# Six weight buffers and four row buffers in the u part of a PEER block, and gate table groups of 16 tokens

## The chip, the cores and the metric

The kernel runs on one core of one Trainium2 chip. The metric is device time in microseconds (us) of one execution. Each kernel has a median over several runs, and one further execution was profiled; all rows come from that one.

## The reference, cut to what matters

The layer is a hybrid attention block (forgetting attention and mLSTM, left out here) followed by PEER, a retrieval over 16384 single-neuron experts. The change is in the PEER half, for 512 tokens of width 2048 in four tiles of 128.

```
D_MODEL, SEQ, PEER_HEADS, PEER_TOPK, PEER_N_KEYS = 2048, 512, 8, 16, 128

def peer_ffn(x, w_q, keys, u, v):                       # x: T=512 tokens x 2048
    q = (xt @ w_q).reshape(T, PEER_HEADS, 2, PEER_KEY_DIM // 2)
    scores = jnp.einsum('thpd,pnd->thpn', q, keys)
    s_top, i_top = lax.top_k(scores, PEER_TOPK)
    cand = s_top[:, :, 0, :, None] + s_top[:, :, 1, None, :]
    s_fin, pos = lax.top_k(cand.reshape(T, PEER_HEADS, 256), PEER_TOPK)
    idx = ...                                           # 8 x 16 = 128 experts per token
    gate = jax.nn.softmax(s_fin, axis=-1)
    act = gelu(sum over d of u[idx] * x) * gate         # u part
    return sum over the 128 experts of act * v[idx]     # v part
```

## The kernel before, in words

**Two ways through PEER.** Tile 0 (128 tokens) and the first 64 tokens of tile 1 go the sparse way: for each of 128 + 64 steps a gather fetches one row of `u` for each of 128 partitions (1 MB, `gathered`, L639, issued on POOL), and VectorE makes its dot product with the token (`dot`, L649). The other 320 tokens go the dense way: all 128 blocks of 128 experts are multiplied with them on TensorE (`early_steps`, tile `sacc`). One block streams two chunks of `uT` (512 KB each), 48 matmuls, a Gelu (tile `es`) and a write to the DRAM table `stab`. Each chunk goes through `stream_split`: SP loads it into `raw` (4 buffers), ScalarE rounds it to `hi` (L117), VectorE makes the remainder `lo` (L119), 3 buffers each. The matmuls take `hi`, then `lo`.

**The gate table.** `table` turns indices and gates of the 384 tokens of tiles 1 to 3 into a table `gtab` in DRAM, `TG` = 32 tokens at a time. I call the work on four tokens a quad: one compare on VectorE (`on`, L949), four scalings on ScalarE (`og`, L954, 6 buffers), matmuls into `gp_` (four calls, eight instructions in the trace), and one copy on ScalarE into `stg` (L957, two buffers). After every 8 quads ScalarE issues the write of `stg` to `gtab` (L961). A quad stands beside three steps of `early_steps`, 18 `sacc` matmuls. Ten groups (80 quads beside 30 blocks) come before the sparse way is done, two groups (16 quads beside 6 blocks) after it, since they need its result.

**Pace.** `advance(n)` runs the sparse steps from inside the dense ones: 1.25 steps per block at first, 1.6 beside the first ten groups (`PACE_G`), and then over 26 blocks as many as are left of `U_STEPS`. A gather is followed by its dot `LAG` = 2 steps later; the pool `rows` has 3 buffers. `beside` makes a gather and a dot wait for the ScalarE `hi` cast that is current in program order.

**The order.** The builder arranges each engine's instructions ahead of time (`lo` with a priority, `AHEAD_LO`), and each engine, SP and POOL too, runs its list strictly in order.

**The stages by time.** To about 920 us attention, output projection and queries; 920 to 963 the end of tile 0's queries (`w_q0`, which reads `x30T`) and its top-k on VectorE; 963 to 1475 queries of the other tiles with 56 blocks; 1515 to 1830 the ten table groups; 1830 to 2045 the 26 blocks with the dense gathers; 2045 to 2110 the last two groups; 2110 to 2200 the last blocks and the loads of gates for the v part (`load_gates`, `gated`, tiles `gtA`, `gtB`); then the v part.

Of the kernel before, what the change touches and what calls it, by code (L numbers as in the profile page):

```python
# [20 lines left out]
P = 128  # L21
# [21 lines left out]
TG = 32  # L43
# [10 lines left out]
LAG = 2  # L54
AHEAD_LO = 35
U_STEPS = SLOTS + S1 + 2 * LAG + 1
# [33 lines left out]
def block_kernel(ctx: ExitStack, tc: tile.TileContext, a, out):  # L90
# [16 lines left out]
    pace = [None]  # L107

    def stream_split(src, width=1024, to=None):
        raw = stream.tile([P, 1024], F32, tag="raw", name="raw", bufs=4)  # L110
# [520 lines left out]
    def gathered(src, idx, n, use, ready):  # L631
        ahead = []
        for j in range(n + LAG):
# [3 lines left out]
            if j < n:  # L637
                row = rows.tile([P, D], F32, tag="row", name="row")
# [4 lines left out]
            if j >= LAG:  # L643
                beside(use(ahead.pop(0), j - LAG))
# [53 lines left out]
    with ExitStack() as rx:  # L698
# [203 lines left out]
        xt0.close()  # L902
        steps = itertools.chain(*[early_steps() for _ in range(EARLY_0)])
# [26 lines left out]
    with ExitStack() as rx:  # L930
# [9 lines left out]
        def table(tg, blocks):  # L940
            stg = n3.tile([P, NI, TG], F32, tag="stg", name="stg")
            steps = itertools.chain(*[early_steps() for _ in range(blocks)])
            for q4 in range(TG // 4):
                for _ in range(blocks):
                    next(steps)
# [6 lines left out]
                for q in range(4):  # L952
# [5 lines left out]
                               in_=gp_)  # L958
            for _ in steps:
                pass  # L960
            nc.scalar.dma_start(out=gtab[tg], in_=stg.rearrange("p i q -> p (i q)"))  # L961

        pace_u[0] = PACE_G
        for tg in range(NS // TG, NTG):
            table(tg, EARLY_G)
# [12 lines left out]
        for tg in range(NS // TG):  # L978
            table(tg, EARLY_G)
# [192 lines left out]
```

## Time and profile before

| | |
|---|---|
| median of 3 runs | 3234.92 us (3233.81 to 3237.32) |
| profiled execution, its own time | 3235.63 us |
| its span, first to last instruction | 3233.8 us |
| TensorE (PE) busy | 3124.3 us, 97% |
| VectorE (DVE) busy | 2324.0 us, 72% |
| ScalarE (ACT) busy | 1277.9 us, 40% |
| mean granted TensorE clock | 0.989 |

The span is 1.8 us less than the execution's own time; the profiled execution lies 0.7 us above the median. Busy PE counts matmuls that overlap in its pipeline, so a stretch in which PE is busy may still run slower than at its best; the number of matmuls in a stretch tells that.

### The profile page before, as it was taken

How to read it: one execution, taken by the hardware profiler on the slowest of the kernel's cores; microseconds unless marked ns; L12 is line 12 of the kernel's file. 1: busy time of each engine (PE TensorE's matmuls, PEld its weight loads, DVE VectorE, ACT ScalarE, POOL GpSimd, SP SyncE). 2: the span in 40 equal slices, each digit the busy share in tenths (PEclk: the TensorE clock that was granted, in tenths of full speed). 3: DMA queues.
4: the chain of work that ended last, by engine and by line, in shares of the span. 5: the costliest groups of instructions: out<-in, count | busy, mean ns of one | idle time of the engine just before them, and what ended most of it. 6: DMA issues, size and time to landing. Idle time of an engine off the chain costs nothing.

```text
span 3233.8 us, 43256 instructions
## 1 busy us (share of the span) xinstructions
PE 3124.3 (97%) x16682; PEld 2746.8 (85%) x16682; DVE 2324.0 (72%) x3251; ACT 1277.9 (40%) x1955; POOL 593.8 (18%) x444
## 2 busy tenths in 40 slices
PE   8999999998989999999999899999999999999998
PEld 6788787787779999999989888997888888888887
DVE  6533333457899999999787888767777777787764
ACT  4432222345443333335777632633333333333332
POOL 0000000100223433322111232121222122221200
PEclk9999999999999999999999999999999999999999
DMA  4232222256868889888888899899888888788753
GB/s 158 72 98 79 78 92 78 79 208 202 311 247 313 315 317 325 321 316 300 332 310 336 337 392 405 300 376 331 300 304 296 305 321 295 291 310 315 274 182 117
DMA packets 220273, 835.71 MB, mean 258 GB/s; under 512 B 21601, under 2 KB 79329, under 8 KB 175969
## 3 DMA queue, kind: packets, MB, share of 16 engines
q1 hardware_dynamic: 153826, 451.24, 41.0%
q0 software_dynamic: 46080, 335.56, 26.7%
q10 hardware_dynamic: 20160, 46.15, 3.7%
q8 instruction: 130, 2.13, 0.3%
q14 instruction: 77, 0.63, 0.1%
HBM read 781.94 MB, written 50.92 MB: 258 GB/s over the span
## 4 chain that ended last, share of the span: by engine, by line
PE 81%; DMA 9%; DVE 5%; ACT 3%; issue 2%; POOL 1%; DVEq 0%; SPq 0%; ACTq 0%; POOLq 0%
PE y L124 24%; PE acc L124 23%; PE sacc L124 20%; PE yk L124 8%; DMA row<-in_u,idx 6%; DVE lo L119 2%; ACT stg L957 1%; ACT og L954 1%; DVE row L649 1%; PE sps L124 1%; DMA raw<-in_w_out 1%; ACT hi L117 1%; PE po L124 1%; DMA raw<-in_w_q 1%; DMA raw<-in_vS 0%
## 5 line engine op out<-in xcount | busy, mean ns | idle before, releaser
L117 ACT CAST hi<-raw 128x1024 fp32r<-128x1024 f32 x736 | 772.6, 1051 | 1487.8 <-PE acc L124 439.8
L119 DVE TENSOR_TENSOR lo<-raw,hi 128x1024 fp32r<-128x1024 f32 x736 | 897.3, 1221 | 584.1 <-ACT hi L117 583.7
L124 PE MATMUL sacc<-x3d,hi 128*128 128x320 f32 x4096 | 925.0, 313 | 5.7 <-ACT hi L117 5.7
L124 PEld LDWEIGHTS sacc<-x3d,hi 128*128 128x128 f32 x4096 | 690.7, 190 | 7.9 <-ACT hi L117 7.9
L124 PE MATMUL sacc<-x3d,lo 128*128 128x320 f32 x2048 | 645.7, 315 | 25.1 <-DVE lo L119 24.5
L649 DVE SCALAR_TENSOR_TENSOR row<-row,x 128x2048 f32<-128x2048 f32 x192 | 438.7, 2286 | 42.7 <-DMA row<-in_u,idx 42.5
L124 PEld LDWEIGHTS sacc<-x3d,lo 128*128 128x128 f32 x2048 | 388.6, 190 | 35.7 <-DVE lo L119 35.6
L639 POOL DMA_INDIRECT row<-in_u,idx x192 | 248.6, 1295 | 701.0 <-ACT hi L117 247.9
L639 POOL DMA_INDIRECT row<-in_v,idx x128 | 217.5, 1699 | 835.3 <-ACT hi L117 601.2
L124 PE MATMUL y<-hi,wbufA 128*128 128x512 f32 x1152 | 357.5, 391 | 4.2 <-ACT hi L117 4.2
L124 PE MATMUL y<-hi,wbufB 128*128 128x512 f32 x1128 | 349.1, 389 | 0.0
L679 DVE SCALAR_TENSOR_TENSOR x<-row,dots,x 128x2048 f32<-128x2048 f32 x128 | 300.0, 2344 | 0.0
L124 PEld LDWEIGHTS y<-hi,wbufA 128*128 128x128 f32 x1152 | 217.2, 189 | 49.7 <-ACT hi L117 4.6
L124 PEld LDWEIGHTS y<-hi,wbufB 128*128 128x128 f32 x1128 | 211.7, 188 | 43.9
L124 PE MATMUL acc<-xT,hi 128*128 128x512 f32 x768 | 244.2, 396 | 0.0
L124 PE MATMUL acc<-hi,xT 128*128 128x512 f32 x768 | 242.0, 393 | 0.0
L124 PE MATMUL y<-lo,wbufA 128*128 128x512 f32 x576 | 225.0, 391 | 1.6 <-DVE lo L119 1.6
L124 PE MATMUL y<-lo,wbufB 128*128 128x512 f32 x564 | 219.4, 389 | 0.0
L164 POOL TENSOR_TENSOR rsr<-rst,mhalf 128x1 f32<-128x1 f32 (+2 forms) x24 | 19.0, 795 | 893.6 <-DVE rst L161 893.6
L124 PEld LDWEIGHTS acc<-xT,hi 128*128 128x128 f32 x768 | 144.1, 189 | 28.5 <-ACT xT L181 0.2
L124 PEld LDWEIGHTS acc<-hi,xT 128*128 128x128 f32 x768 | 143.9, 188 | 28.6
L949 DVE TENSOR_TENSOR on<-cst,idxT 128x1024 f32<-128x1024 f32 x96 | 117.0, 1221 | 65.4 <-PE gp__19012 L124 5.9
(545 smaller groups left out, 4204.4 us busy)
## 6 DMA issues: line engine op xcount, KB each, us to landing
raw<-in_uT SPq DMA_DIRECT2D x256, 512.0 KB, 6.9
raw<-in_vS SPq DMA_DIRECT2D x256, 512.0 KB, 4.4
raw<-in_w_out SPq DMA_DIRECT2D x64, 512.0 KB, 4.3
raw<-in_w_q SPq DMA_DIRECT2D x64, 512.0 KB, 5.2
gtab<-stg ACTq DMA_DIRECT2D x12, 2048.0 KB, 12.6
stab<-es ACTq DMA_DIRECT2D x128, 160.0 KB, 6.5
sv<-stab SPq DMA_DIRECT2D x64, 320.0 KB, 7.9
raw<-in_w_fqk SPq DMA_DIRECT2D x32, 512.0 KB, 3.5
```

The costliest lines, as they stand in the source:

```text
L117: pace[0] = nc.scalar.copy(out=hi[:, :width], in_=raw[:, :width]).ins
L119: nc.vector.tensor_tensor(out=lo[:, :width], in0=raw[:, :width], in1=hi[:, :width].bitcast(F32), op=OP.subtract)
L124: nc.tensor.matmul(out=o, lhsT=l, rhs=r, start=start, stop=stop)
L164: nc.gpsimd.tensor_tensor(out=r, in0=t, in1=mhalf[:, 0:width], op=OP.pow)
L639: beside(nc.gpsimd.indirect_dma_start(out=row, out_offset=None, in_=a[src], in_offset=bass.IndirectOffsetOnAxis(ap=idx(j), axis=0)))
L649: return nc.vector.scalar_tensor_tensor(out=row, in0=row, scalar=1.0, in1=x30, op0=OP.mult, op1=OP.mult, accum_out=to[:, j:j + 1])
L679: return nc.vector.scalar_tensor_tensor(out=x2[:, 0, :], in0=row, scalar=dots[0][:, j:j + 1], in1=x2[:, 0, :], op0=OP.mult, op1=OP.add)
L949: nc.vector.tensor_tensor(out=on, in0=iota[:, None, None, :].to_broadcast([P, 2, 4, P]), in1=idxT[:, :, t4:t4 + 4, None].to_broadcast([P, ...
L954: nc.scalar.activation(out=og, in_=on[:, 0, q, :], func=AF.Copy, scale=gT[:, t4 + q:t4 + q + 1])
L957: nc.scalar.copy(out=stg[:, :, q4 * 4:q4 * 4 + 4].rearrange("p i q -> p q i"), in_=gp_)
```

## The change

`stream_split` takes two of every six chunks to a new tag `rawx` with 2 buffers, and `gathered` takes every fourth row to `rowx` with 1 buffer, in a pool `more` that is opened when `x30T` is closed (16 KB a partition) and closed after the table groups; `more[0]` is set to None before the last two (now four) groups. While it is open, a dot follows its gather 3 steps later (`LAG_U`) instead of 2; `U_STEPS` grows by 2. `TG` becomes 16: groups of 4 quads, so 24 writes of 1 MB instead of 12 of 2 MB, and gates are later loaded in runs of 512 bytes instead of 1024. The number of quads, blocks and gathers is the same, and so is the pattern of three steps to a quad.

```
--- before.py
+++ after.py
@@ -40,7 +40,7 @@
 DU = ND - NS
 NI = 128
 GB = 8
-TG = 32
+TG = 16
 FIRST_HEADS = 4
 EARLY_0 = 2
 EARLY_TOPK = (2, 2, 3)
@@ -52,8 +52,9 @@
 PACE_G = 1.6
 PACE_HOLD = 1.0
 LAG = 2
+LAG_U = 3
 AHEAD_LO = 35
-U_STEPS = SLOTS + S1 + 2 * LAG + 1
+U_STEPS = SLOTS + S1 + 2 * LAG_U + 1
 NTG = ND // TG
 
 
@@ -105,9 +106,14 @@
     x2 = const.tile([P, NT, D], F32, name="x2")
 
     pace = [None]
+    more, chunks = [None], [0]
 
     def stream_split(src, width=1024, to=None):
-        raw = stream.tile([P, 1024], F32, tag="raw", name="raw", bufs=4)
+        chunks[0] += 1
+        if more[0] and chunks[0] % 6 >= 4:
+            raw = more[0].tile([P, 1024], F32, tag="rawx", name="rawx", bufs=2)
+        else:
+            raw = stream.tile([P, 1024], F32, tag="raw", name="raw", bufs=4)
         nc.sync.dma_start(out=raw[:, :width], in_=src)
         if to is None:
             hi = stream.tile([P, 1024], F32R, tag="hi", name="hi", bufs=3)
@@ -630,18 +636,25 @@
 
     def gathered(src, idx, n, use, ready):
         ahead = []
-        for j in range(n + LAG):
+        lag, used = LAG, [0]
+        for j in range(n + LAG_U):
+            if more[0] and src == "u":
+                lag = LAG_U
             while j < n and not ready(j):
                 done[0] -= 1
                 yield
             if j < n:
-                row = rows.tile([P, D], F32, tag="row", name="row")
+                if lag == LAG_U and j % 4 == 3:
+                    row = more[0].tile([P, D], F32, tag="rowx", name="rowx", bufs=1)
+                else:
+                    row = rows.tile([P, D], F32, tag="row", name="row")
                 beside(nc.gpsimd.indirect_dma_start(
                     out=row, out_offset=None, in_=a[src],
                     in_offset=bass.IndirectOffsetOnAxis(ap=idx(j), axis=0)))
                 ahead.append(row)
-            if j >= LAG:
-                beside(use(ahead.pop(0), j - LAG))
+            if len(ahead) > lag or (j >= n and ahead):
+                beside(use(ahead.pop(0), used[0]))
+                used[0] += 1
             yield
 
     def dot(to):
@@ -900,6 +913,8 @@
         for _ in scores0:
             pass
         xt0.close()
+        ux = ctx.enter_context(ExitStack())
+        more[0] = tpool(ux, "more", side="right")
         steps = itertools.chain(*[early_steps() for _ in range(EARLY_0)])
         pace_u[0] = PACE_EARLY
         for _ in steps:
@@ -937,11 +952,10 @@
                 nc.tensor.transpose(pt[:, (t - 1) * P:t * P], flat(src[:, t]), ident)
             nc.scalar.copy(out=dst, in_=pt)
 
-        def table(tg, blocks):
+        def table(tg, steps):
             stg = n3.tile([P, NI, TG], F32, tag="stg", name="stg")
-            steps = itertools.chain(*[early_steps() for _ in range(blocks)])
             for q4 in range(TG // 4):
-                for _ in range(blocks):
+                for _ in range(EARLY_G):
                     next(steps)
                 gp_ = psB.tile([P, 4, NI], F32, tag="ps", name="gp_")
                 t4 = tg * TG + q4 * 4
@@ -956,13 +970,18 @@
                     mm(gp_[:, q, :], on[:, 1, q, :], og, True, True)
                 nc.scalar.copy(out=stg[:, :, q4 * 4:q4 * 4 + 4].rearrange("p i q -> p q i"),
                                in_=gp_)
+            nc.scalar.dma_start(out=gtab[tg], in_=stg.rearrange("p i q -> p (i q)"))
+
+        def tables(tgs):
+            steps = itertools.chain.from_iterable(
+                early_steps() for _ in range(EARLY_G * len(tgs) * TG // 32))
+            for tg in tgs:
+                table(tg, steps)
             for _ in steps:
                 pass
-            nc.scalar.dma_start(out=gtab[tg], in_=stg.rearrange("p i q -> p (i q)"))
 
         pace_u[0] = PACE_G
-        for tg in range(NS // TG, NTG):
-            table(tg, EARLY_G)
+        tables(range(NS // TG, NTG))
         pace_u[0] = max(0.0, U_STEPS - done[0]) / (NI - HOLD - nearly[0])
         while nearly[0] < NI - HOLD:
             early_s()
@@ -975,8 +994,9 @@
         for r in range(R):
             rs = slice(r * S1, (r + 1) * S1)
             nc.scalar.copy(out=gT[rs, 0:NS], in_=pt[rs, r * NS:(r + 1) * NS])
-        for tg in range(NS // TG):
-            table(tg, EARLY_G)
+        more[0] = None
+        tables(range(NS // TG))
+    ux.close()
 
 
     va = tpool(ctx, "va", 2)
```

The change also moves instructions, because the builder arranges them anew. ACT, around a group border in the first table part, before: the rows follow the one that issues a group's write, and `gp__n` is the psum tile of one quad.

```order
L957 COPY stg<-gp__14847 128x4x128
L954 ACTIVATE og<-on,gT 128x128 x2
L611 ACTIVATE es<-sacc 128x320
L954 ACTIVATE og<-on,gT 128x128
L957 COPY stg<-gp__14890 128x4x128
L612 DMA stab<-es 128x320
L954 ACTIVATE og<-on,gT 128x128 x5
L957 COPY stg<-gp__14937 128x4x128
L954 ACTIVATE og<-on,gT 128x128 x2
L117 CAST hi<-raw 128x1024
L957 COPY stg<-gp__14971 128x4x128
```

The change, on ACT, around a border of the same stretch:

```order
L971 COPY stg<-gp__14774 128x4x128
L968 ACTIVATE og<-on,gT 128x128 x4
L123 CAST hi<-raw 128x1024
L617 ACTIVATE es<-sacc 128x320
L971 COPY stg<-gp__14814 128x4x128
L618 DMA stab<-es 128x320
L973 DMA gtab<-stg 128x2048
L968 ACTIVATE og<-on,gT 128x128 x6
L971 COPY stg<-gp__14857 128x4x128
L968 ACTIVATE og<-on,gT 128x128 x2
L123 CAST hi<-rawx 128x1024
L971 COPY stg<-gp__14900 128x4x128
```

Before, four copies of quads follow one another with one `hi` cast among them, after a stretch in which PE's list has 49 to 57 `sacc` rows between the ends of two quads; in the change the border is every fourth quad, that stretch is 24 to 37 rows, and casts stand between the copies. Counted over PE's lists by the `sacc` rows between the ends of quads: four quads in a row end within 22 rows in 21 places of before and in one of the change (evenly spaced they would take 54). Two quads in a row end less than 10 rows apart in 35 places before (32 of them in the first ten groups) and in 15 of the change (14).

SP, where the first blocks of the dense way are loaded (about 919 to 932 us), before:

```order
L111 DMA raw_7156<-in_w_q 128x1024
L111 DMA raw_7215<-in_uT 128x1024
L111 DMA raw_7273<-in_uT 128x1024
L111 DMA raw_7341<-in_uT 128x1024
L111 DMA raw_7399<-in_uT 128x1024
L111 DMA raw_7487<-in_w_q 128x1024
L111 DMA raw_7517<-in_w_q 128x1024
L111 DMA raw_7550<-in_w_q 128x1024
L111 DMA raw_7580<-in_w_q 128x1024
```

The change:

```order
L117 DMA raw_7156<-in_w_q 128x1024
L117 DMA raw_7218<-in_uT 128x1024
L117 DMA raw_7401<-in_uT 128x1024
L117 DMA raw_7489<-in_w_q 128x1024
L117 DMA raw_7519<-in_w_q 128x1024
L117 DMA rawx_7275<-in_uT 128x1024
L117 DMA rawx_7343<-in_uT 128x1024
L117 DMA raw_7552<-in_w_q 128x1024
L117 DMA rawx_7582<-in_w_q 128x1024
```

The second and third chunk of `uT`, `raw_7273` and `raw_7341` before and `rawx_7275` and `rawx_7343` now, have moved behind the fourth chunk and two chunks of `w_q`; the first of them waits for PE, for the last read of `x30T`.

SP, where the last blocks and the first v chunks are loaded (about 2147 to 2155 us), before:

```order
L111 DMA raw_19746<-in_uT 128x1024
L111 DMA raw_19776<-in_uT 128x1024
L997 DMA sv_19879<-stab_4822 128x2x320
L111 DMA raw_19813<-in_uT 128x1024
L997 DMA sv_19886<-stab_4822 128x2x320
L997 DMA sv_19965<-stab_4822 128x2x320
L111 DMA raw_19843<-in_uT 128x1024
L988 DMA gtA_19322<-gtab_4823 128x12x256
L111 DMA raw_19914<-in_vS 128x1024
```

The change:

```order
L1017 DMA sv_19907<-stab_4822 128x2x320
L117 DMA raw_19774<-in_uT 128x1024
L1017 DMA sv_19914<-stab_4822 128x2x320
L1017 DMA sv_19993<-stab_4822 128x2x320
L117 DMA raw_19804<-in_uT 128x1024
L1008 DMA gtA_19350<-gtab_4823 128x24x128
L117 DMA raw_19841<-in_uT 128x1024
L117 DMA raw_19871<-in_uT 128x1024
L117 DMA raw_19942<-in_vS 128x1024
```

The load of `gtA` for the third gate group, of 1.5 MB, has moved ahead of the last two `uT` chunks, and is in 3072 runs instead of 1536.

## Rows read from the trace of the kernel before

**Rows 1.** The page, lines of its parts 1, 3, 5 and 6.

```profile
PE 3124.3 (97%) x16682; PEld 2746.8 (85%) x16682; DVE 2324.0 (72%) x3251; ACT 1277.9 (40%) x1955; POOL 593.8 (18%) x444
...
q1 hardware_dynamic: 153826, 451.24, 41.0%
q0 software_dynamic: 46080, 335.56, 26.7%
...
L649 DVE SCALAR_TENSOR_TENSOR row<-row,x 128x2048 f32<-128x2048 f32 x192 | 438.7, 2286 | 42.7 <-DMA row<-in_u,idx 42.5
...
raw<-in_uT SPq DMA_DIRECT2D x256, 512.0 KB, 6.9
```

**Rows 2.** Busy time by stretch (us; number of instructions), granted clock, DMA share.

```profile
core 0: us, PE busy (x) PEld busy (x) DVE busy (x) ACT busy (x) POOL busy (x), PEclk, DMA share, GB/s
920.00:963.00 43.00, 31.02 (x195) 29.89 (x194) 42.42 (x122) 16.07 (x24) 12.64 (x11) 0.88 0.61 218
963.00:1475.00 512.00, 512.00 (x3366) 510.34 (x3365) 480.63 (x1045) 177.49 (x231) 183.23 (x146) 1.00 0.89 317
1515.00:1830.00 315.00, 294.17 (x2010) 281.76 (x2009) 255.69 (x224) 236.64 (x483) 55.71 (x44) 0.99 0.84 317
1830.00:2045.00 215.00, 195.38 (x1246) 185.26 (x1245) 175.94 (x156) 65.08 (x83) 59.80 (x48) 0.98 1.00 394
2110.00:2200.00 90.00, 79.41 (x461) 73.68 (x460) 54.27 (x42) 30.59 (x43) 18.28 (x10) 0.94 0.96 352
2200.00:3150.00 950.00, 950.00 (x4193) 786.64 (x4192) 714.07 (x600) 306.30 (x348) 188.22 (x112) 1.00 0.82 295
```

**Rows 3.** The chain of waits, 2045 to 2086 us (start, us, what).

```profile
2055.95 2.64 PE sacc L124 x18
2058.59 0.89 PE gp__18769 L124 x8
```

**Rows 4.** Timeline of ACT at one group border, 1670 to 1692 us.

```profile
1679.43 1.12 ACT L957 COPY stg<-gp__15184 128x512 f32<-128x512 f32 x1 [4.95 <-PE gp__15184 L124]
...
1681.57 1.06 ACT L957 COPY stg<-gp__15227 128x512 f32<-128x512 f32 x1
...
1682.43 1.54 ACT L954 ACTIVATE og<-on,gT 128x128 f32<-128x128 f32 x5
1683.97 1.05 ACT L957 COPY stg<-gp__15271 128x512 f32<-128x512 f32 x1
...
1686.33 1.07 ACT L957 COPY stg<-gp__15308 128x512 f32<-128x512 f32 x1
...
1689.29 1.12 ACT L957 COPY stg<-gp__15351 128x512 f32<-128x512 f32 x1
```

**Rows 5.** Waits of PE, 1515 to 1830 us (us in total, times, longest).

```profile
PE sacc L124 <- ACT hi L117: 4.0, 9, 0.4
PE gp__14634 L124 <- ACT og L954: 0.8, 1, 0.8
```

**Rows 6.** The tile gtab: time from issue to landing of its DMAs (2 MB writes among them).

```profile
DMA to landing us min/median/max: 8.8/12.8/16.2
```

**Rows 7.** DMA of the stretch 1850 to 2025 us (40 slices, then all).

```profile
GB/s 410 355 353 390 421 419 382 375 372 428 317 327 385 402 414 410 406 413 409 419 424 406 407 421 419 393 374 394 420 411 393 407 416 413 420 381 387 406 421 411
DMA packets 15205, 69.70 MB, mean 398 GB/s; under 512 B 1694, under 2 KB 4390, under 8 KB 9863
```

**Rows 8.** Timelines of SP and PE, 915 to 960 us.

```profile
918.87 8.77 SPq L111 DMA_DIRECT2D raw<-in_uT  x4
...
929.77 0.28 PE L124 MATMUL acc<-hi,x30T 128*128 128x256 f32 x1
...
958.57 0.69 PE L124 MATMUL acc<-x3d,lo 128*128 128x384 f32 x1 [7.39 <-DVE lo L119]
```

**Rows 9.** Timelines of SP and ACT, 2160 to 2200 us.

```profile
2174.34 0.43 SPq L988 DMA_DIRECT2D gtB<-gtab  x1
...
2189.93 0.50 ACT L1005 COPY wv<-gtB 128x128 f32<-128x128 f32 x2 [12.56 <-DMA gtB<-gtab]
```

More of the change, by code (lines that the diff above doesn't have):

```diff
@@ L42 @@
 GB = 8
-TG = 32
+TG = 16
 FIRST_HEADS = 4
@@ L54 @@
 LAG = 2
+LAG_U = 3
 AHEAD_LO = 35
-U_STEPS = SLOTS + S1 + 2 * LAG + 1
+U_STEPS = SLOTS + S1 + 2 * LAG_U + 1
 NTG = ND // TG
@@ L107, in block_kernel @@
     pace = [None]
+    more, chunks = [None], [0]
     def stream_split(src, width=1024, to=None):
-        raw = stream.tile([P, 1024], F32, tag="raw", name="raw", bufs=4)
+        chunks[0] += 1
+        if more[0] and chunks[0] % 6 >= 4:
+            raw = more[0].tile([P, 1024], F32, tag="rawx", name="rawx", bufs=2)
+        else:
+            raw = stream.tile([P, 1024], F32, tag="raw", name="raw", bufs=4)
         nc.sync.dma_start(out=raw[:, :width], in_=src)
@@ L632, in gathered @@
         ahead = []
-        for j in range(n + LAG):
+        lag, used = LAG, [0]
+        for j in range(n + LAG_U):
+            if more[0] and src == "u":
+                lag = LAG_U
             while j < n and not ready(j):
@@ L637, in gathered @@
             if j < n:
-                row = rows.tile([P, D], F32, tag="row", name="row")
+                if lag == LAG_U and j % 4 == 3:
+                    row = more[0].tile([P, D], F32, tag="rowx", name="rowx", bufs=1)
+                else:
+                    row = rows.tile([P, D], F32, tag="row", name="row")
                 beside(nc.gpsimd.indirect_dma_start(
@@ L642, in gathered @@
                 ahead.append(row)
-            if j >= LAG:
-                beside(use(ahead.pop(0), j - LAG))
+            if len(ahead) > lag or (j >= n and ahead):
+                beside(use(ahead.pop(0), used[0]))
+                used[0] += 1
             yield
@@ L902, in block_kernel @@
         xt0.close()
+        ux = ctx.enter_context(ExitStack())
+        more[0] = tpool(ux, "more", side="right")
         steps = itertools.chain(*[early_steps() for _ in range(EARLY_0)])
@@ L938, in block_kernel, with table @@
             nc.scalar.copy(out=dst, in_=pt)
-        def table(tg, blocks):
+        def table(tg, steps):
             stg = n3.tile([P, NI, TG], F32, tag="stg", name="stg")
-            steps = itertools.chain(*[early_steps() for _ in range(blocks)])
             for q4 in range(TG // 4):
-                for _ in range(blocks):
+                for _ in range(EARLY_G):
                     next(steps)
@@ L958, in table, with tables @@
                                in_=gp_)
+            nc.scalar.dma_start(out=gtab[tg], in_=stg.rearrange("p i q -> p (i q)"))
+        def tables(tgs):
+            steps = itertools.chain.from_iterable(
+                early_steps() for _ in range(EARLY_G * len(tgs) * TG // 32))
+            for tg in tgs:
+                table(tg, steps)
             for _ in steps:
                 pass
-            nc.scalar.dma_start(out=gtab[tg], in_=stg.rearrange("p i q -> p (i q)"))
         pace_u[0] = PACE_G
-        for tg in range(NS // TG, NTG):
-            table(tg, EARLY_G)
+        tables(range(NS // TG, NTG))
         pace_u[0] = max(0.0, U_STEPS - done[0]) / (NI - HOLD - nearly[0])
@@ L977, in block_kernel @@
             nc.scalar.copy(out=gT[rs, 0:NS], in_=pt[rs, r * NS:(r + 1) * NS])
-        for tg in range(NS // TG):
-            table(tg, EARLY_G)
+        more[0] = None
+        tables(range(NS // TG))
+    ux.close()
     va = tpool(ctx, "va", 2)
```

## The prediction, made before the changed kernel was run

> **What bounds the kernel now.** I read the page first. TensorE is busy 97% of the span [rows 1], so anything to be won lies in the stretches where it waits or runs below its best pace, and I looked for these with the table of stretches [rows 2]. From 963 to 1475 us, while the sparse gathers already run, PE is busy 512 of 512 us at full granted clock, and so it is from 2200 to 3150: more buffers can win nothing there. The change touches four stretches where it is not so: 920 to 963 (PE busy 31 of 43 us, clock 0.88), 1515 to 1830 (294 of 315), 1830 to 2045 (195 of 215) and 2110 to 2200 (79 of 90). The two long ones have different bounds, and this decides the forecast.
>
> In the dense gathers, 1830 to 2045 us, the DMA engines are busy at a share of 1.00 at 394 GB/s [rows 2]; in the middle of it, 398 GB/s, with slices between 317 and 428 [rows 7]. VectorE is idle 39 of 215 us; its dots wait 42.5 us for gathered rows in the whole kernel [rows 1], nearly all of it here. `lo` stands behind these dots in its queue, and PE waits for `lo`. This looks like too few row buffers, but the transfers have no idle time left: bytes bound it.
>
> In the table part, 1515 to 1830 us, the DMA share is 0.84, VectorE is busy 255.7 and ScalarE 236.6 of 315 us [rows 2]: no engine is full, and PE still loses time. How much: where quads are evenly spaced, later in the same program, 18 `sacc` matmuls take 2.64 us and a quad's eight matmuls 0.89 us with nothing between [rows 3], 3.53 us for both. The 80 quads of this part need 80 x 3.53 = 282 us so; they take 315. The loss is 33 us, 3.3 per group. The timeline shows where it arises [rows 4]: between two copies ScalarE sits idle 4.95 us, waiting for a quad whose last matmuls stand behind a stretch of `sacc` in PE's list (49 rows from the end of the quad before); then five quads come at once. Their copies start at 1679.43, 1681.57, 1683.97, 1686.33 and 1689.29, every 2.1 to 3.0 us, since each quad needs four scalings (five take 1.54 us, about 0.31 each) and a copy of 1.05 to 1.12. PE's own work between these copies is 0.89 us plus 0, 2 or 5 `sacc` of 0.147: 0.9 to 1.6. It waits for `og` up to 0.8 us at a time and for `hi` in nine places [rows 5]. So the order of the list makes this loss, not a full engine: PE first runs ahead without quads, then ScalarE cannot make them as fast as they are asked for.
>
> **The change, part by part.** (1) *The order of the table part.* With groups of 16 tokens the long stretch in PE's list is 24 to 37 rows instead of 49 to 57, and the clusters are pairs instead of fours. I price each gap between two quads as the larger of PE's work and ScalarE's 2.3 us (the mean of the three shortest distances of copies, 2.14, 2.40 and 2.36, in [rows 4]). By this rule the 32 close gaps of before (11 of 5 rows at 0.67, one of 3 at 0.97, 12 of 2 at 1.12, eight of none at 1.41) cost 33 us, as much as is lost. The 14 close gaps of the change: seven of 5 rows at 0.67, one of 2 at 1.12, two of 7 at 0.4, three of 6 at 0.5, one of 8 at 0.2, together 8.3 us. For runs of three quads 10 to 12 rows apart, into which casts fall, I add 2.5. So 33 - 11 = 22 us are won. Bounds: 33 if all the waits go, nothing if a pair costs what a cluster did. I take 20, because VectorE and the DMA get closer to full: 255.7 us of work in 295 (87%), 0.84 x 315 = 265 (90%). The last two groups have one cluster (three close gaps, 5, 3 and 2 rows: 0.7 + 1.0 + 1.1) and get one pair (0.7): 2 us won, bounds 0 and 3.
>
> (2) *Twelve more writes of the table*, 1 MB each, on ScalarE's queue. SP's issue of a gate load takes 0.43 us [rows 9]; at that, they are 5 us in all, hidden under ScalarE's idle time (78 of 315 us). Without that cover they would cost those 5. A copy into `stg` now has to wait for the write two groups back, issued five quads earlier, 5 x 3.53 = 17.6 us, instead of nine, 31.8. A 2 MB write lands after 8.8 to 16.2 us [rows 6], so a write of half the size is in time: nothing.
>
> (3) *Six weight buffers.* Two more chunks are in flight, 1 MB that is moved before the bytes-bound stretch instead of in it: 1.05 MB at 398 GB/s is 2.6 us won there. In the table part PE's waits for `hi` are 4.0 us in all [rows 5], and part (1) holds them.
>
> (4) *The fourth row and the lag of 3.* When tile 0's gathers end, its dots need one more step before the next gathers start, so one gather more (1.05 MB, 2.6 us) falls into the dense stretch; and `U_STEPS` is two steps longer over the same 26 blocks, so the gathers are a little denser and end about half a block earlier, after which PE can run at its own 7.04 us a block (48 x 0.147): some 1 us more. (3) and (4) together: 1 us lost; bounds 11 won, if the DMA ran all the while at the 424 GB/s of its good slices (6% of 190 us), and 5 lost.
>
> The Trainium skill, in "DMA: Bandwidth & Descriptors", section Bandwidth, puts the ceiling of the 16 engines' ports at 435 GB/s and that of one core's share of the HBM at about 358. The trace goes past the second figure, 398 GB/s over 175 us, so that does not bind here; by the first, the 190 us of dense gathers could shrink by an estimated 8.5%, 16 us.
>
> (5) *The first extra buffers.* `rawx_7275`, second chunk of the first block, is issued when PE has read `x30T` for the last time, at 930 us; before, the four `uT` chunks were issued between 919 and 928 [rows 8]. It lands some 7 us later (median 6.9 [rows 1]) and is then cast, so PE gets it at 938 where it asked at about 935: 3 us later, with `w_q` chunks and gathers behind it on SP and POOL. But in this stretch VectorE is the bound, busy 42.4 of 43 us [rows 2], and PE waits for it later anyway, up to 7.4 us at once [rows 8]. There the lag takes dots off the way: in VectorE's list four dots stand ahead of the fourth `lo` of `w_q` before, two in the change, 2 x 2.3 us [rows 1]. Sum nothing; bounds 4 either way.
>
> (6) *Gates in runs of 512 bytes.* 1536 more packets a load. From the page's two queues [rows 1]: 138 ns for a packet of 2.9 KB, 300 ns for one of 7.3 KB, so by a line through them 29 ns fixed to a packet, 2.8 us per load over 16 engines. In the v part 2.8 in some 65 us is hidden, DMA share 0.82 [rows 2]. From 2110 to 2200 the share is 0.96 and the gate load is on the chain: ScalarE waits 12.6 us for `gtB` and the next `hi` stands behind it [rows 9]. Three loads lie there: from nothing to 8 us; I take 2, since the weights' packets, smaller than the gathers', do not show the full fixed price as idle PE. That `gtA` moved ahead of two `uT` chunks only swaps who waits in a queue that is full either way.
>
> Sum: -20 - 2 + 0 + 1 + 0 + 2 = -19 us. Against the profiled execution's own 3235.6 us that gives 3216.6; the median of before lies 0.7 lower, so 3216.
>
> **The rivals.** *Half the gain:* the pairs are still paid for, because `hi`, `es` and the DMA issues stand between a pair's scalings; 10 us less, 3226. For it: in evenly filled lists casts come at any place; against: in rows 4 the copies come every 2.1 to 2.4 us with such work between.
>
> *The dense gathers gain too:* the waits for rows go with the fourth buffer, 11 us more, 3205. For it: those 39 us of idle VectorE; against: the DMA share of 1.00. The Trainium skill, "Perfetto Trace Analysis", section Optimization Strategy, says that a bubble that repeats on the engine that should be full can mean too little on-chip memory for the next tile, buffer counts named first; this stretch looks just like that, and by that rule alone all 20 us of idle PE would go.
>
> *No change:* the table part is won and then handed on to the stretch behind it. For this the dense gathers would have to depend on transfers made during PE's idle time in the table part. Only four `raw` and three rows can be ahead, and at 0.84 share they already are. 3235.
>
> *Slower:* the place of the old wait is taken by one for the table's write. Each of 22 groups then waits at its first copy for the write two groups back; it starts to cost when 1 MB needs over 17.6 us to land, and decides at 18.6, where 22 x 1 us has eaten the gain. At 19 us it costs 22 x 1.4 = 31: 3247. Against it: 16.2 us is the longest landing of twice the size [rows 6].
>
> **How the numbers follow.** Forecast 52%, half the gain 16%, dense gathers too 12%, no change 10%, slower 10%. The forecast's own range is 3206 to 3225. The whole range, 3202 to 3234, leaves out the slower case, half of the dense gathers' and some of no change. A difference under 0.2%, 6.5 us, can hardly be told from none in this kernel. Faster by more: 52 + 12 + most of 16 = 76%; within: 13%; slower: 11%.
>
> **What would show it.** Right: the stretch of the ten groups' quads takes 290 to 300 us instead of 315, ScalarE's idle pieces of 4 to 6 us before a copy are gone, and PE's waits for `og` are rare; the dense stretch stays near 215 us at a DMA share of 1.00. Wrong: waits of ScalarE's copies for `gtab` writes; a table part still above 308 us; dense gathers below 205 us with the DMA at 415 GB/s or more; a gap of PE over 5 us near 935 us that is not made good by 963.

## The result, and the profile after

The change runs in 3191.73 us, the median of four runs (3191.11 to 3194.7), against 3236.12 us before in the same comparison: a ratio of 0.9867, 95% interval 0.9855 to 0.9880. That is 44.4 us less, where the prediction had 19 less and a range that ended at 3202. The profiled execution took 3191.11 us, its span is 3189.3.

The page of the change, lines of its parts 1, 3 and 5, to be held against [rows 1]:

```profile
PE 3108.9 (97%) x16682; PEld 2737.0 (86%) x16682; DVE 2324.3 (73%) x3251; ACT 1274.7 (40%) x1955; POOL 604.5 (19%) x444
...
q1 hardware_dynamic: 178402, 451.24, 41.9%
...
L662 DVE SCALAR_TENSOR_TENSOR row<-row,x 128x2048 f32<-128x2048 f32 x147 | 336.2, 2288 | 20.2 <-DMA row<-in_u,idx 20.1
```

The same number of matmuls, and 15.4 us less of busy PE: part of the time that was won had been counted as busy. So the share of 97%, as large as before, says nothing; the stages do. Busy time by stretch in the change, the answer to [rows 2]:

```profile
913.00:956.00 43.00, 35.53 (x238) 33.44 (x237) 42.83 (x123) 19.66 (x29) 13.06 (x11) 0.92 0.77 276
956.00:1468.00 512.00, 512.00 (x3366) 510.35 (x3366) 483.11 (x1048) 177.59 (x231) 181.25 (x146) 1.00 0.89 316
1508.00:1793.00 285.00, 281.16 (x2010) 274.39 (x2009) 254.89 (x225) 234.68 (x484) 66.10 (x44) 1.00 0.94 351
1795.00:2003.00 208.00, 195.47 (x1260) 185.89 (x1259) 179.10 (x159) 64.75 (x81) 64.23 (x49) 0.99 1.00 408
```

The 2010 matmuls that took 315 us in the table part now fit in 285. To measure stages alike in all kernels I use the `es` activations: each ends a block, and I number the blocks from 0. The view of the tile `es` on ScalarE gives the first and last start in a window and the number of them. Before, for blocks 57 to 87 (table part), 87 to 113 (dense gathers) and 113 to 121 (last groups):

```profile
L611 ACT ACTIVATE es<-sacc x31: 414/433/479, 1506.3 to 1832.6; 128x320 f32<-128x320 f32 x31
L611 ACT ACTIVATE es<-sacc x27: 427/430/438, 1832.6 to 2049.5; 128x320 f32<-128x320 f32 x27
L611 ACT ACTIVATE es<-sacc x9: 416/432/446, 2049.5 to 2123.3; 128x320 f32<-128x320 f32 x9
```

The change:

```profile
L617 ACT ACTIVATE es<-sacc x31: 412/435/504, 1499.2 to 1795.6; 128x320 f32<-128x320 f32 x31
L617 ACT ACTIVATE es<-sacc x27: 423/431/433, 1795.6 to 2003.2; 128x320 f32<-128x320 f32 x27
L617 ACT ACTIVATE es<-sacc x9: 418/432/438, 2003.2 to 2074.5; 128x320 f32<-128x320 f32 x9
```

So the table part went from 326.3 to 296.4 (29.9 won), the dense gathers from 216.9 to 207.6 (9.3), the last groups from 73.8 to 71.3 (2.5). The first stage is read from PE's last matmul with `x30T`, ahead of which the change moves nothing: 929.77 before [rows 8], 927.26 after. That difference of 2.5 us is one of executions, since several of the kernels below, alike up to there, have it between 922.8 and 928.9. From it to the `es` of block 2 it took 58.0 us before and 53.4 after: 4.6 won. From block 2 to block 57 nothing changed (518.5 and 518.6). From block 121 to the end of the span it is 1110.5 before and 1114.8 after: 4.3 lost. 2.5 + 4.6 + 29.9 + 9.3 + 2.5 - 4.3 = 44.5, the difference of the spans.

Where the waits went: in the table part PE's waits for `og`, 35 of them before, most of 0.5 to 0.8 us as the one in [rows 5], are now twelve (16.9 us in all before, 3.5 now), and those for `hi` are gone. The waits of PE from 1508 to 1793 us, the first two lines:

```profile
PE gp__13886 L130 <- ACT og L968: 1.0, 1, 1.0
PE gp__15578 L130 <- ACT og L968: 0.3, 1, 0.3
```

In the dense gathers the DMA is steady. The DMA of the change from 1830 to 1975 us, 40 slices and their sum, against [rows 7]:

```profile
GB/s 420 423 415 409 425 418 420 421 411 420 416 420 418 422 417 420 416 416 418 418 413 415 422 414 431 404 424 410 426 418 416 419 410 425 411 429 414 417 415 420
DMA packets 13200, 60.60 MB, mean 418 GB/s; under 512 B 1477, under 2 KB 3862, under 8 KB 8503
```

No slice is below 404, where before they fell to 317. Near the end of the stretch a new wait stands, one remainder behind a dot whose row lands late. Timelines of PE and DVE, 1974 to 1991 us:

```profile
1983.27 0.44 PE L130 MATMUL sacc<-x3d,lo 128*128 128x320 f32 x1 [4.20 <-DVE lo L125]
1979.78 2.29 DVE L662 SCALAR_TENSOR_TENSOR rowx<-rowx,x 128x2048 f32<-128x2048 f32 x1 [1.67 <-DMA rowx<-in_u,idx]
1981.99 1.22 DVE L125 TENSOR_TENSOR lo<-raw,hi 128x1024 fp32r<-128x1024 f32 x1
```

At the entry to the v part ScalarE now waits for the first gates as well as for the second ones, and PE for the cast behind. Timelines of ACT and PE, 2080 to 2150 us, against [rows 9]:

```profile
2084.74 0.30 ACT L1025 COPY wv<-gtA 128x128 f32<-128x128 f32 x1 [9.83 <-DMA gtA<-gtab]
2144.08 0.50 ACT L1025 COPY wv<-gtB 128x128 f32<-128x128 f32 x2 [13.12 <-DMA gtB<-gtab]
2088.44 0.56 PE L130 MATMUL sacc<-x3d,hi 128*128 128x320 f32 x2 [4.24 <-ACT hi L123]
```

### The profile page after: what moved, and what is told of

Read it like the earlier page. It is cut to its first block, busy times and chain, and to the rows that moved or that the text cites. A ratio compares the mean times of both kernels' runs of the same rounds, so it can differ in the third digit from the quotient of the medians.

```text
span 3189.3 us, 43251 instructions
## 1 busy us (share of the span) xinstructions
PE 3108.9 (97%) x16682; PEld 2737.0 (86%) x16682; DVE 2324.3 (73%) x3251; ACT 1274.7 (40%) x1955; POOL 604.5 (19%) x444
## 4 chain that ended last, share of the span: by engine, by line
PE 83%; DMA 7%; DVE 6%; issue 2%; ACT 2%; POOL 1%; SPq 0%; DVEq 0%; ACTq 0%; POOLq 0%
PE y L130 24%; PE acc L130 24%; PE sacc L130 20%; PE yk L130 8%; DMA row<-in_u,idx 4%; DVE lo L125 2%; DMA rowx<-in_u,idx 2%; DVE row L662 1%; PE sps L130 1%; PE po L130 1%; DMA sv<-stab 1%; ACT stg L971 1%; DMA gtB<-gtab 1%; ACT hi L123 1%; DMA raw<-in_uT 0%
## 5 line engine op out<-in xcount | busy, mean ns | idle before, releaser
L125 DVE TENSOR_TENSOR lo<-raw,hi 128x1024 fp32r<-128x1024 f32 x649 | 790.6, 1220 | 583.2 <-ACT hi L123 582.7
L123 ACT CAST hi<-raw 128x1024 fp32r<-128x1024 f32 x649 | 681.4, 1050 | 1295.9 <-PE y L130 388.3
L662 DVE SCALAR_TENSOR_TENSOR row<-row,x 128x2048 f32<-128x2048 f32 x147 | 336.2, 2288 | 20.2 <-DMA row<-in_u,idx 20.1
L651 POOL DMA_INDIRECT row<-in_u,idx x147 | 194.8, 1325 | 500.0 <-ACT hi L123 222.2
L123 ACT CAST hi<-rawx 128x1024 fp32r<-128x1024 f32 x87 | 91.2, 1051 | 175.3 <-PE sacc L130 102.2
```

The costliest lines, as they stand in the source:

```text
L651: beside(nc.gpsimd.indirect_dma_start(out=row, out_offset=None, in_=a[src], in_offset=bass.IndirectOffsetOnAxis(ap=idx(j), axis=0)))
L662: return nc.vector.scalar_tensor_tensor(out=row, in0=row, scalar=1.0, in1=x30, op0=OP.mult, op1=OP.mult, accum_out=to[:, j:j + 1])
```

## The experiments

My theory after the result: the order won the table part, for a close pair of quads costs almost nothing; the fourth row, not the weight buffers, made the DMA steady; the lag won the first blocks; the short packets lost the end. The rivals stand with each run. All stages of the profiled executions, in us, and the medians (A: last matmul with `x30T` to block 2; B: blocks 57 to 87; C: 87 to 113; D: block 121 to the end of the span). Each profiled execution is one of its kernel's runs and need not be a typical one. The ratios are to the runs of before that were taken beside these, whose medians were 3236.12 for the change, 3237.79 for e1 to e4, 3236.11 for e5 to e8 and 3234.78 for e9 to e12:

| kernel | median (runs) | ratio to before, 95% | A | B | C | D |
|---|---|---|---|---|---|---|
| before | 3236.12 | | 58.0 | 326.3 | 216.9 | 1110.5 |
| the change | 3191.73 | 0.9855 to 0.9880 | 53.4 | 296.4 | 207.6 | 1114.8 |
| e1 groups alone | 3196.99 (3196.47 to 3201.85) | 0.9862 to 0.9894 | 58.7 | 295.8 | 212.3 | 1114.6 |
| e2 and raw 6 | 3200.96 (3191.9 to 3202.67) | 0.9876 to 0.9909 | 58.5 | 296.0 | 209.8 | 1111.6 |
| e3 and row 4, lag 3 | 3189.77 (3188.37 to 3190.75) | 0.9840 to 0.9873 | 53.0 | 297.4 | 207.8 | 1114.9 |
| e4 og 4 | 3191.36 (3187.89 to 3192.34) | 0.9841 to 0.9874 | 55.0 | 297.3 | 207.1 | 1114.9 |
| e5 row 4, lag 2 | 3190.40 (3187.89 to 3190.74) | 0.9838 to 0.9871 | 58.7 | 296.9 | 203.7 | 1115.4 |
| e6 og 2 | 3215.93 (3212.78 to 3217.97) | 0.9922 to 0.9955 | 53.3 | 315.5 | 211.6 | 1113.4 |
| e7 layout | 3221.28 (3212.92 to 3222.79) | 0.9929 to 0.9963 | 55.2 | 329.2 | 211.5 | 1108.7 |
| e8 pace 1.8 | 3183.95 (3183.21 to 3185.41) | 0.9822 to 0.9855 | 54.9 | 313.0 | 190.5 | 1114.0 |
| e9 split lag | 3190.24 (3186.8 to 3191.68) | 0.9842 to 0.9875 | 53.9 | 296.7 | 206.3 | 1115.9 |
| e10 and pace 1.7 | 3184.43 (3182.66 to 3185.26) | 0.9828 to 0.9861 | 53.2 | 300.0 | 200.2 | 1114.5 |
| e11 and pace 1.9 | 3179.44 (3172.41 to 3181.06) | 0.9802 to 0.9840 | 53.0 | 309.3 | 189.3 | 1114.7 |
| e12 pace 1.7, raw 6 | 3183.65 (3182.31 to 3186.38) | 0.9828 to 0.9861 | 54.1 | 299.3 | 197.7 | 1113.0 |

**e1, the groups alone** (both extra tags off):

```
-        if more[0] and chunks[0] % 6 >= 4:
+        if False:
-                if lag == LAG_U and j % 4 == 3:
+                if False:
-LAG_U = 3
+LAG_U = 2
```

> The groups of 16 tokens alone: four weight buffers, three rows and a lag of 2 as before. Theory A (the parts add, stage by stage): the table part takes what it takes in the changed kernel, about 296 us from the 57th to the 87th block instead of 326, the last groups save 2.5, the v part's start costs 4 as it does there, and the dense gathers and the first blocks stay as before; in all some 28 us faster than before, 3208. Rival B (the extra buffers carry half of what the table part won, since weights and rows that came too late were part of its loss): table part near 310 us, in all some 14 us faster, 3222.

Theory A holds in the table part (295.8), the first blocks and the end; rival B falls. In all e1 is 11 us faster than A had it: the groups alone bring the median 40.8 us below that of before. The profiled execution, the slowest of its four, is 33.7 below. So stages are those of one execution, and medians decide between kernels.

The groups of 16 change the order and halve each write of the table, and no run parts the two. But no copy into `stg` waits for a write in the table part, before or after, so the traces leave the order as the cause there.

The dense gathers won 4.6 us, which A had not. What the DMA moved from block 87 to block 113, in all and on ScalarE's queue (q10), first before, then e1:

```profile
DMA packets 18292, 85.06 MB, mean 392 GB/s; under 512 B 2036, under 2 KB 5241, under 8 KB 11855
q10 hardware_dynamic: 3749, 6.20, 7.5%
```

```profile
DMA packets 18204, 83.52 MB, mean 393 GB/s; under 512 B 2016, under 2 KB 5219, under 8 KB 11822
q10 hardware_dynamic: 3747, 5.15, 6.5%
```

The rate is the same, but 1.54 MB less were moved, which are 3.9 us at 393 GB/s. 1.05 MB of it is on ScalarE's queue: the last write of the ten groups is issued just behind block 87 in both, and it is 1 MB now instead of 2.

**e2, the weight buffers** (as e1, but `rawx` stays) **and e3, the row with its lag** (`rowx` and `LAG_U = 3`, no `rawx`):

> Groups of 16 and the six weight buffers; three rows, lag 2. Theory A (the fourth row and the lag win the dense gathers, the weight buffers only the first blocks): dense gathers 216 us from the 87th to the 113th block as before, 913 to 956 us some 4 to 7 us shorter, in all 3202 to 3205. Rival B (what kept the DMA queues from being full was the weights): dense gathers 208 us, in all 3192 to 3200. Rival C (the weight buffers do nothing): as the groups of 16 alone.

> Groups of 16, the fourth row and the lag of 3; four weight buffers. Theory A (rows win the dense gathers): 208 us from the 87th to the 113th block, DMA at 415 GB/s or more in it; the first blocks keep about half of their 7 us, since the lag takes two dots of 2.3 us ahead of w_q's remainder; in all 3196 to 3200. Rival B (the weights win it): 216 us and 398 GB/s, in all 3205 or more.

The fourth row does it. DMA from 1830 to 1975 us, the line of the sum, first e2, then e3:

```profile
DMA packets 12735, 58.52 MB, mean 404 GB/s; under 512 B 1411, under 2 KB 3715, under 8 KB 8203
```

```profile
DMA packets 13154, 60.59 MB, mean 418 GB/s; under 512 B 1453, under 2 KB 3801, under 8 KB 8464
```

With three rows and six weight buffers slices still fell to 311. None of e2's theories held as a whole: its dense gathers are nearer B (209.8), its time is no better than e1's, as C has it, with runs 11 us apart. The profiled one, 3191.9, is the fastest of the four by 7 us, so its 404 GB/s and 209.8 us may be better than what the kernel does as a rule. Its first blocks show what the prediction called the late `rawx`: the first `es` comes 16.7 us after the last matmul with `x30T` instead of 10.8, but block 2 ends no later (58.5). e3 has the stages that A expected, the first blocks even better, and is as fast without the weight buffers as the whole change.

**e5, the row without the lag:**

```
-                if lag == LAG_U and j % 4 == 3:
+                if more[0] and src == "u" and j % 4 == 3:
-LAG_U = 3
+LAG_U = 2
```

> Groups of 16 and the fourth row, but with the lag of 2; four weight buffers. It parts the row from the lag. Theory A (three gathers in flight beside one dot need the lag as well: with a lag of 2 VectorE still asks for a row two steps after its issue): dense gathers stay near 212 us at 397 to 404 GB/s as with three rows, VectorE's waits for rows stay above 33 us, 3196 or more. Rival B (the buffer alone does it): 208 us at 418 GB/s, waits for rows near 25 us, 3188 to 3192. For the first blocks: theory A, the gain of some 5 us goes with the lag, since it is the lag that moves dots behind w_q's remainder; rival B, it stays.

The two theories are each right in one place. For the dense gathers theory A falls: the buffer alone makes the DMA steady, at the same 418 GB/s from 1830 to 1975 us:

```profile
DMA packets 13150, 60.60 MB, mean 418 GB/s; under 512 B 1466, under 2 KB 3794, under 8 KB 8453
```

From block 87 to block 113, first e5, then the change:

```profile
DMA packets 18210, 83.37 MB, mean 409 GB/s; under 512 B 2031, under 2 KB 5263, under 8 KB 11836
```

```profile
DMA packets 18498, 84.79 MB, mean 408 GB/s; under 512 B 2050, under 2 KB 5378, under 8 KB 11980
```

e5 moves as much as e1, faster: 8.6 us (212.3 to 203.7) for the buffer alone. The change moves 1.42 MB more at the same rate and takes 3.9 us longer; part (4) of the prediction had one gather more falling into this stretch.

For the first blocks theory A stands: 58.5 to 58.7 us with the lag of 2 (e1, e2, e5), 53.0 to 55.2 with 3 (all the others).

**e9, the lag of 3 for tile 0 alone** (`if more[0] and src == "u" and n == SLOTS:`, with the row of e5, four weight buffers):

> Groups of 16, four weight buffers, the fourth row, and a lag of 3 for tile 0's gathers but 2 for tile 1's; U_STEPS one step shorter than in the change. Theory A (the lag of 3 wins the first blocks and costs in the dense gathers, the row buffer wins the dense gathers): first blocks as with lag 3, some 5 us shorter than with lag 2, dense gathers near 204 us as with lag 2 instead of 208; 3185 to 3188. Rival B (the 204 us of the run with lag 2 came from the gathers that lag 2 had already made before the 87th block, not from the lag in the stretch): dense gathers 207 us or more, 3189 to 3192.

Nearer rival B. The first blocks are as with lag 3, and the dense gathers 206.3 against 207.8 in e3. POOL issues 47 gathers of `u` in this stretch in e5, but 48 in e9 and in the change, so the 203.7 of e5 came mostly of one gather more made ahead of it: e9 moves 84.38 MB at the same 409 GB/s, and 1.01 MB more is 2.5 of the 2.6 us. What is left for the lag is 1.5 us, one execution each; the wait of 4.2 us at the end is there in e3 too, and not in e9.

**e4 and e6, fewer `og` buffers in the change** (`bufs=6` to 4 and to 2). PE's list is nearly that of the change in e4, and another one in e6.

> The changed kernel with four og buffers instead of six, so that ScalarE can make no scaling of the quad after next ahead; 12 close pairs of quads in PE's list instead of 14. Theory A (pairs cost nothing because ScalarE has made scalings ahead during the long stretch before them): each pair pays up to the 2.3 us less PE's work, some 0.5 us, and the table part is 5 to 8 us longer, 3197 to 3200. Rival B (pairs cost nothing for another reason, or two quads are never asked for faster than ScalarE makes them): table part within 1 us, 3191 to 3192.

> The changed kernel with two og buffers instead of six: ScalarE can be no more than half a quad ahead; the builder then puts six close pairs in PE's list instead of 14. Theory A (a pair is free because ScalarE makes scalings ahead, and four buffers were still enough for that): PE now waits for og at most quads, some 0.3 us each, table part 10 to 25 us longer, 3202 to 3216. Rival B (scalings ahead play no part, PE's matmuls of a quad stand among those of sacc and leave ScalarE time for each): table part within 3 us of the changed kernel.

With four, nothing (296.4 to 297.3), as rival B had it, though ScalarE waits for PE to give back a buffer 8 times, 14.5 us in all. With two, 19 us in the table part and 24.2 by the medians, since some quads are now made only behind block 87 and the last groups lose 4.6 us as well. ScalarE then waits for a buffer 49 times in the table part, 42.1 us in all, and in the change never. So scalings made ahead are worth these 24 us, and one quad's are enough. e6 has another order and six close pairs instead of 14, so it shows that the stage needs scalings ahead, but not what a single pair costs. The stage and the longest such wait in e6:

```profile
L617 ACT ACTIVATE es<-sacc x31: 413/428/440, 1494.7 to 1810.2; 128x320 f32<-128x320 f32 x31
```

```profile
ACT og L968 <- PE gp__16208 L130: 2.9, 1, 2.9
```

How a pair goes in the change is seen on ACT, 1680 to 1689 us (quads `gp__15535` and `gp__15578`):

```profile
1681.07 0.99 ACT L968 ACTIVATE og<-on,gT 128x128 f32<-128x128 f32 x3 [0.23 <-ACT og L968]
1684.31 0.69 ACT L968 ACTIVATE og<-on,gT 128x128 f32<-128x128 f32 x2 [2.24 <-DVE on L963]
1685.14 1.08 ACT L971 COPY stg<-gp__15535 128x512 f32<-128x512 f32 x1
1686.01 0.69 ACT L968 ACTIVATE og<-on,gT 128x128 f32<-128x128 f32 x2
1686.59 1.05 ACT L123 CAST hi<-rawx 128x1024 fp32r<-128x1024 f32 x1
1687.53 1.10 ACT L971 COPY stg<-gp__15578 128x512 f32<-128x512 f32 x1
```

The copies are 2.39 us apart, as in [rows 4]. But the first quad's scalings and two of the second's were made before the first copy, and PE doesn't wait for the copy. It lost 0.3 us here, the second line of its waits above.

**e7, another layout of the gate table:**

```
-    gtab = gdram.tile([NTG, P, NI * TG], F32, name="gtab")
+    gtab = gdram.tile([NI // GB, P, NTG, GB * TG], F32, name="gtab")
...
-            nc.scalar.dma_start(out=gtab[tg], in_=stg.rearrange("p i q -> p (i q)"))
+            nc.scalar.dma_start(out=gtab[:, :, tg].rearrange("g p x -> p g x"),
+                                in_=stg.rearrange("p (g i) q -> p g (i q)", i=GB))
...
-                          in_=gtab[tgs, :, g * GB * TG:(g + 1) * GB * TG].rearrange("g p x -> p g x"))
+                          in_=gtab[g, :, tgs])
```

> The changed kernel with the gate table in another layout in DRAM, by gate group, then partition, then token group: a load of gates is then in runs of 12 KB (8 KB and 4 KB for the split first load), and each write of the table is in runs of 512 bytes instead of 8 KB. The order of instructions on PE is the same. Theory A (the 4.4 us lost from the 121st block to the end come from gates in runs of 512 bytes): 4 to 6 us less there, and the table part, whose DMA share is 0.94, loses at most 2: 3186 to 3189. Rival B (they come from the order of SP's list, the load of gtA ahead of two uT chunks): no difference at the end, 3191 to 3195.

At the end theory A: 6.1 us less (1108.7), less even than before the change, with the same order on every engine. The size is less sure than the sign, since the kernels with runs of 512 bytes lie between 1111.6 (e2) and 1115.9 (e9): 3 to 7 us. The waits of ScalarE for gates in e7, against those of the change:

```profile
2120.57 0.30 ACT L1026 COPY wv<-gtA 128x128 f32<-128x128 f32 x1 [9.26 <-DMA gtA<-gtab]
2176.49 0.50 ACT L1026 COPY wv<-gtB 128x128 f32<-128x128 f32 x2 [9.55 <-DMA gtB<-gtab]
```

The new wait for `gtA` stays with long runs, so it does not come from the short ones; the wait for `gtB` is 3.6 us shorter.

But the short runs are now in the table's writes, and the table part lost 33 us instead of 2. The timeline of ACT in e7, 1595 to 1684 us, shows how:

```profile
1595.25 0.38 ACTq L973 DMA_DIRECT2D gtab<-stg  x1
...
1619.06 1.01 ACT L971 COPY stg<-gp__14687 128x512 f32<-128x512 f32 x1 [5.45 <-DMA gtab<-stg]
1619.08 2.41 ACTq L618 DMA_DIRECT2D stab<-es  x1
...
1682.10 1.03 ACT L971 COPY stg<-gp__15365 128x512 f32<-128x512 f32 x1 [2.21 <-DMA gtab<-stg]
1682.18 3.91 ACTq L618 DMA_DIRECT2D stab<-es  x1
```

This is the prediction's slower rival, though the layout brings it about and not the groups: the copy waits for the write two groups back, which needs 23.8 us here (1595.25 to 1619.06), past the 17.6 from which it costs. The issue of a small write on the same queue takes 2.41 and 3.91 us too, instead of 0.33, and holds up the scalings behind it. Of the two this is the larger: the waits of ScalarE from 1506 to 1825 us, the first two lines.

```profile
ACT og L968 <- issue: 19.3, 7, 6.2
ACT stg L971 <- DMA gtab<-stg: 10.1, 3, 5.5
```

And TensorE's clock adds to it. The table part in e7 and in the change:

```profile
1498.00:1827.20 329.20, 302.29 (x2081) 294.28 (x2080) 266.55 (x239) 242.34 (x494) 66.31 (x46) 0.96 0.91 318
1499.20:1795.60 296.40, 292.56 (x2080) 285.77 (x2079) 265.26 (x239) 240.76 (x495) 67.44 (x46) 0.99 0.94 350
```

The granted clock is 0.96 instead of 0.99: behind four of its waits for `og`, the longest of 5.4 us, PE ran at the lower of its two levels, 1.2 GHz, for a while. 3% of 329 us are some 10 of the 33 us, an estimate.

**e8, a faster pace beside the table groups** (`PACE_G = 1.8` in the change):

> The changed kernel with PACE_G 1.8 instead of 1.6: six gathers and dots move from the 26 dense blocks into the 30 blocks beside the table groups, where DMA moved 351 GB/s and VectorE was busy 255 of 285 us. Theory A (the dense gathers are bound by bytes, the table part has room for them): dense gathers 6 x 2.5 = 15 us shorter, 193 us, table part up to 2 longer; 3176 to 3180. Rival B (VectorE at 269 of 285 us delivers the remainders late, and 19 close pairs instead of 14 add to it): the table part gives back 6 to 15 us, 3184 to 3193.

Both were half right: the dense gathers won 17.1 us, so bytes do bound them, and the table part gave back 16.6; 3.9 more came between blocks 30 and 57 (246.1 us instead of 250.0). In e8 and e11 the first quad's matmuls come 18.3 us behind block 57 instead of 9.4, so part of what the table part gave back is a later start. All stages together are 3.7 us better than the change's, the medians 7.8.

**e10, e11 and e12** (e9 with `PACE_G` 1.7, 1.9, and 1.7 with six weight buffers):

> The kernel with the split lag and PACE_G 1.7: three gathers move out of the dense blocks into the table part; 14 close pairs of quads in PE's list and no four quads within 22 rows, where PACE_G 1.8 had 19 and one. Theory A (what PACE_G 1.8 lost in the table part was the order at its start, and VectorE has room): table part 294 to 298 us, dense gathers 7 us shorter than with the split lag alone, 3178 to 3182. Rival B (each gather moved into the table part costs there what it wins later, since VectorE is nearly full): table part some 7 us longer, no gain, 3185 to 3189.

> The kernel with the split lag and PACE_G 1.9: nine gathers move. Close pairs 15, four quads within 22 rows nowhere, but a start of the table part like that of PACE_G 1.8. Theory A (order at the start costs some 9 us, VectorE at 275 of 285 us has just room): table part 305 to 309, dense gathers 186 us, close to what PE needs alone for 26 blocks (26 x 7.04 = 183); 3174 to 3180. Rival B (VectorE full): table part 315 us or more, 3184 or more.

> As the split lag with PACE_G 1.7, but with the six weight buffers as well. Theory A (with the fourth row there the weight buffers add nothing): within 2 us of the same kernel with four. Rival B (they keep the DMA queues fuller in the dense gathers): 3 us or more faster.

With 1.7 the table part took 300.0 and the dense gathers 200.2: 5.8 us faster than e9 by the medians, between A and B. With 1.9 it is theory A, 309.3 and 189.3, and the fastest kernel of all: 3179.44 us, a ratio to before of 0.9821 (0.9802 to 0.9840), and 12 us below the change, whose interval doesn't meet its. Its stretches, the table part without its start and the dense gathers:

```profile
1545.00:1804.00 259.00, 251.92 (x1768) 241.71 (x1767) 240.00 (x214) 206.01 (x422) 69.51 (x45) 1.00 0.97 378
1804.00:1993.00 189.00, 186.86 (x1266) 184.97 (x1265) 159.81 (x142) 67.94 (x88) 70.53 (x41) 1.00 1.00 402
```

In the first one VectorE is busy 240 of 259 us and the DMA 0.97, in the second PE 186.9 of 189: no stage has much left to give to another. e12 is as fast as e10: with the row there, the weight buffers add nothing.

## Why the prediction was wrong

The stages won 44.5 us where the sum had 19. Of the 25.5 between them 10.3 lie in the dense gathers (1 lost by the sum, 9.3 won), 9.9 in the table part (20 and 29.9), 4.6 in the first blocks (0 and 4.6), 0.5 in the last groups and 2.5 in the execution; the gates took back 2.3.

**The term for the table part was mis-sized.** The place, the mechanism and the sign were right: e1 changes the groups alone and gets all of the 30 us. The step that failed is "I price each gap between two quads as the larger of PE's work and ScalarE's 2.3 us". That rule was calibrated on runs of four and five quads, where ScalarE works without a pause and so sets the pace; it seemed to fit the loss, and I then used it for single pairs. A pair is the case in which ScalarE still has the scalings of the first quad and part of the second's ready. The 14 pairs were priced at 8.3 us and the runs of three at 2.5; in the change the waits for `og` in the whole part are one of 1.0 and some of 0.2 and 0.3, 3.5 us in all. The discount of 2 us for a fuller VectorE and DMA was not needed either. The loss itself was read too small. 282 us is the price of 2080 matmuls (80 quads of 8, 30 blocks of 48), but the 315 us hold 2010 of them [rows 2]. At the same pace these need 273, so some 42 us were lost, not 33; that the rule gave 33 too was chance, and so is it that 29.9 stays inside a bound of 33. The change takes 285 us for 2010 matmuls, 12 above that pace.

**The dense gathers: the step "bytes bound it" was wrong for the kernel before.** A share of 1.00 did not mean that the engines moved all they could: at that same share they moved 397 to 404 GB/s with three rows (e1, e2) and 418 with four (e3, e5, e9), from 1830 to 1975 us. The slices down to 317 were in [rows 7], and I used them for a bound only. Bytes bind it now, and e8 shows it: six gathers of 1.05 MB are 15 us at 418 GB/s, and without them the stretch is 17.1 shorter. The bound of 11 us and the rival were in the text, at 12%. The Trainium skill, "Perfetto Trace Analysis", section Optimization Strategy, spoke for that rival: a bubble that repeats can mean too few buffers. The runs agree as to the buffer (8.6 us from e1 to e5), not as to all 20 us of idle PE. The Trainium skill, on the same page, section Identifying the Most-Contended Engine, says that the occupancy of 16 DMA engines misleads and that HBM utilization, a rate, is to be used for them; 397 and 418 GB/s at one and the same share agree. The 9.3 us add up so: 4.6 came without any buffer (e1), 3.9 of them since 1.54 MB less had to be moved, while the prediction put the smaller writes at nothing; 8.6 came with the row (e1 to e5); 3.9 were given back with the rest of the change, 2.6 of them by one gather more, as part (4) had it.

**The first blocks: right reasons, a wrong sum.** Both effects that I named are there: `rawx` makes the first block late (16.7 us instead of 10.8 in e2), and the lag moves dots off the way to `w_q`'s remainders. I set them off against each other at 0 ±4. But VectorE is the bound, by the argument that I gave myself, so two dots of 2.3 us off its way count: 4.6 us won, and 2.8 to 5.0 in all the kernels with the lag of 3. The late block costs little: the stage takes 53.0 to 53.9 us with four weight buffers, 53.3 to 55.2 with six.

**The gates were mis-sized:** 2 lost, bounds 0 to 8; measured 4.3, and 6.1 more than with long runs (e7). The wait for `gtA`, 9.83 us above, had no part in my count, since I looked at `gtB` alone; but e7 has it too and ends sooner, so it is not where the time goes.

**Right in size** were the last groups (2 predicted, 2.5 measured), twelve more writes at no cost (ScalarE never waits for one in the change), nothing from 963 to 1475 us, and the late first block. The 2.6 us that the weight buffers were to win can't be told from nothing: e12 is 0.8 us below e10, the change 2 above e3.

## What to carry to other kernels

A price taken from a cluster, where one engine works without pause, doesn't hold for a pair: ask how much the engine can have made ahead when the pair is reached, and where the answer hangs on a buffer count, count it. A DMA share of 1.00 did not say here that transfers moved at the best rate (393 and 409 GB/s, e1 and e5 apart by one buffer); look at the spread of its slices, and where they dip, try one more buffer before bytes are called the bound. Count the bytes of a stage before its rate is compared: e1 won there by moving less. When two effects meet in a stage, ask first which of them touches the engine that bounds it: here that one counted nearly alone.

## What the runs showed of the hardware

- At a DMA share of 1.00 the rate was 397 to 404 GB/s with three rows and a steady 418 (slices 404 to 431) over 145 us with four.
- A write of 1 MB in runs of 512 bytes to DRAM took up to 23.8 us beside gathers, until the copy that waited for it could start, and such writes cost the table part 33 us; loads in runs of 512 bytes cost the v part's entry 6.1 us against runs of 12 KB, one execution each. ScalarE's queue (q10) from 1590 to 1640 us (packets, MB, share of 16 engines), in e7 and in the change:

```profile
q10 hardware_dynamic: 6429, 3.64, 24.4%
q10 hardware_dynamic: 1152, 3.97, 19.5%
```

  In the time that its packets took, that is 298 GB/s with runs of 512 bytes and 407 with runs of 8 KB, by estimate. The Trainium skill, "DMA: Bandwidth & Descriptors", section Specifications, names 512 bytes as the least transfer for the line rate; here writes of that size did not reach what longer ones did.
- The issue of a 160 KB write on ScalarE's queue, 0.33 us as a rule, took 1.14 to 7.17 us ten times in e7, the one kernel with such writes.
- One more megabyte of buffers was worth 6.6 us as a row (e1 to e5, by the medians; 8.6 in the dense gathers of the profiled executions), and nothing that can be told as two weight buffers (e10 to e12).
